# Attention output: weights as the stationary operand, with ones beside the values

## The chip, the cores and the metric

The kernel runs on one core of a Trainium2 chip. The metric is the device time of one execution in microseconds (us). The core has a matrix engine (TensorE; the profile calls its matmuls PE and its loads of stationary operands PEld), a vector engine (DVE), a scalar engine (ACT), GpSimd (POOL) and DMA queues, of which nearly all work here is issued by SP. Each engine executes its own instructions strictly in the order in which the program lists them, and waits on semaphores for what it needs from the others.

## The reference

One layer of a hybrid encoder runs over two requests, a prompt of 256 tokens and a sample of 2048, each with 1024 features. A projection feeds two mixers, a Hyena mixer (two long convolutions by transforms, 512 channels) and a dilated attention (8 heads of 64). Their outputs are normalised, concatenated and projected; then comes a gated feed-forward layer. The change touches the attention, which runs three branches over the same queries, with dilations 1, 4 and 16, and merges them by their softmax denominators:

```
s = jnp.einsum('brnqhe,brnkhe->brnhqk', qb, kb).astype(jnp.float32) * (E ** -0.5)
...
s = jnp.where(valid[None, None, :, None], s + bias[None, None, None], NEG_INF)
m = jnp.max(s, axis=-1, keepdims=True)
p = jnp.exp(s - m)
den = jnp.sum(p, axis=-1)
o = jnp.einsum('brnhqk,brnkhe->brnqhe', p, vb.astype(jnp.float32)) / jnp.swapaxes(den, -1, -2)[..., None]
lse = jnp.swapaxes(m[..., 0] + jnp.log(den), -1, -2)
...
wts = jax.nn.softmax(jnp.stack(lses, axis=0), axis=0)
o = jnp.sum(wts[..., None] * jnp.stack(outs, axis=0), axis=0)
```

So for every query, head and branch three things are needed: the unnormalised sum of weights times values (64 numbers), the extreme score `m`, and the denominator `den`.

## The kernel before

The stages follow each other: input projection and Hyena filters, Hyena with the rest of the projection, attention woven with Hyena, output projection, feed-forward. `mixers` (lines 1052 to 1118) writes attention and Hyena as two generators and `weave` alternates their steps by the rates in line 1050 (`at=440`, `h2=90`). That fixes the order in which the code is emitted. The context is built with `schedule_with_timeline_sim=True` (line 1690): a scheduler then reorders what was emitted, by its own estimate of when each instruction can start, and lists one static order per engine. The order that an engine really executes can therefore move wherever an instruction is added, removed or judged cheaper.

Attention works on pairs of heads (`hp`, four of them), three branches (`b`) and blocks of 128 queries: 54 blocks per pair, 216 in all. One block goes through these steps:

- `scores` (line 874): four matmuls (lines 902, 903; two heads, a high and a low part of the queries) write scores `aS` in PSUM; DVE adds the bias and finds the minimum (line 906; the scores are negated); ACT takes the exponential into `aP` (line 909), and with `accum_out` also the denominator.
- `flip` (line 912): TensorE transposes the weights (line 918, tile `aT`), DVE or ACT copies them to `aPT`.
- `values` (line 928): for each head, the values (`aV`, 64 columns) are the stationary operand and the transposed weights, 128 columns, are moved past them (line 933). The two heads write the lower and upper 64 partitions of `aOp`. A block whose window has two chunks of keys takes four matmuls, one with one chunk two; each fp32 matmul shows as two records in the profile, so 1408 in all.
- After the last block of a group of up to four, ACT copies `aOp` to `aOC` (line 938), `tokens` (line 942) transposes it back to query rows on TensorE (line 946), DVE copies them to `aO` (line 947), and a DMA stores `aO` with minimum and denominator in columns 128 to 131.

Two chunks are of 128 keys each, except at the two ends of a sequence or residue class: there one of the two has 64. There are 88 blocks with two full chunks, 48 with a full and a half one, and 80 with one chunk.

Hyena (line 748) runs its second stage, `hyena_second` (line 696), in 32 steps per convolution of the sample: three fp32 matmuls of 512 columns (lines 721, 725, 739), five DVE operations (lines 723, 729 to 732), a POOL addition (733) and an ACT copy (742). Then 16 steps of the last stage follow (lines 769 to 783): load `hD` from DRAM, two matmuls side by side (line 776, two records each), one DVE multiplication (777), store of the result. All 16 of these steps must be done before the second 256 token rows of the output projection can start, because each step writes rows that are spread over the whole sample. The first 256 rows (the prompt) do not need them.

`merged_rows` (line 1121) later loads the stored rows and merges the branches; `om` (lines 206 to 208 there) is the output projection.

Of the kernel before, what the change touches and what calls it, by code (L numbers as in the profile page):

```python
# [13 lines left out]
F32 = mybir.dt.float32  # L14
F32R = mybir.dt.float32r
AF = mybir.ActivationFunctionType
# [12 lines left out]
REQ = ((0, LP), (LP, LS))  # L29
DILS = (1, 4, 16)  # L30


# [155 lines left out]
class Hybrid:  # L188
# [607 lines left out]
    def attention_groups(self, b, rs):  # L796

        dil = DILS[b]
        out = []
        for r in rs:  # L800
            off, L = REQ[r]
            ls = L // dil
            if ls >= 256:
                nb = ls // P
                out += [(r, "win", [(res, j, nb) for j in range(j0, min(nb, j0 + 4))])
                        for res in range(dil) for j0 in range(0, nb, 4)]
            elif ls == P:
                out += [(r, "res", [(res, 0, 1) for res in range(g, g + 4)]) for g in range(0, dil, 4)]
            else:
                out.append((r, "pack", [(0, j, L // P) for j in range(L // P)]))  # L810
        return out

    def attention_values(self, wp, b, cs):

        nc = self.nc
        dil = DILS[b]
        vt = wp.tile([P, 22, P], F32, tag="aV", name="aV", bufs=2)
        av = self.tok["av"][:, cs]
# [3 lines left out]
        for r in (1, 0):  # L822
# [20 lines left out]
            else:  # L843
                ld(vt[:, n:n + 2], av[off:off + L].rearrange("(p s) k -> p s k", s=2))
                n += 2
        return vt, base

# [22 lines left out]
    def attention(self, wp, psS, psT, psO, first, mq):  # L870
        nc, a = self.nc, self.a
        q1, q2, q3 = [], [], []

        def scores(heads, g, i, blk, ot, bias, b):
# [4 lines left out]
            ps = psS.tile([P, 2, 256], F32, tag="aS", name="aS")  # L879
            sb = wp.tile([P, 2, 256], F32, tag="aP", name="aP", bufs=2)  # L880
            for hh in range(2):
# [22 lines left out]
            for hh in range(2):  # L904
                mn, dn = ot[:, i, 128 + hh:129 + hh], ot[:, i, 130 + hh:131 + hh]
                nc.vector.tensor_tensor_reduce(out=sb[:, hh, :n], in0=ps[:, hh, v0:v0 + n],  # L906
                                               in1=bias[:, hh, b0:b0 + n], scale=1.0, scalar=3e38,
                                               op0=ALU.add, op1=ALU.min, accum_out=mn)
                nc.scalar.activation(sb[:, hh, :n], sb[:, hh, :n], AF.Exp, scale=-1.0, bias=mn, accum_out=dn)  # L909
            return sb, n  # L910
# [16 lines left out]

        def values(x):
            po, vt, i, pe, ch = x["po"], x["vt"], x["i"], x["pe"], x["ch"]
            for c, (c0, cn) in enumerate(ch):  # L930
                for hh in range(2):
                    hs = slice(64 * hh, 64 * hh + 64)
                    nc.tensor.matmul(po[hs, i], vt[:cn, x["v"] + c * x["vs"], hs], pe[:cn, hh, c],
                                     start=(c == 0), stop=(c == len(ch) - 1))
            if x["last"]:
                n = i + 1
                oc = wp.tile([P, 4, P], F32, tag="aOC", name="aOC", bufs=1)
                nc.scalar.copy(oc[:, :n], po[:, :n])
                x["oc"] = oc
                q3.append(x)  # L940

        def tokens(x):
            ot, n = x["ot"], x["i"] + 1
            pt = psT.tile([P, 4, P], F32, tag="aT", name="aOT")
            for i in range(n):
                nc.tensor.transpose(pt[:, i], x["oc"][:, i], self.ident)
            nc.vector.tensor_copy(ot[:, :n, 0:P], pt[:, :n])
            x["store"]()

# [34 lines left out]
        for hp in range(4):  # L984
# [6 lines left out]
            for b in range(3):  # L991
# [6 lines left out]
                for g in self.attention_groups(b, (0, 1) if hp == 3 else (1, 0)):  # L998
                    r, kind, blks = g
                    ot = wp.tile([P, 4, 132], F32, tag="aO", name="aO", bufs=3)  # L1000
                    po = psO.tile([P, 4, P], F32, tag="aOp", name="aOp")
                    for i, blk in enumerate(blks):
# [15 lines left out]
                        if len(q1) > 1:  # L1018
# [3 lines left out]
                            yield  # L1022
                        if q3:
                            tokens(q3.pop(0))
                        if len(q2) > 1:
# [6 lines left out]
        for y in q2:  # L1032
            values(y)
            while q3:
                tokens(q3.pop(0))
        op = self.pool(mq, "o_b", side="left")
# [84 lines left out]
    def merged_rows(self, wp, mg, c0):  # L1121
# [5 lines left out]
        for i in range(2):  # L1127
            rows = slice(c0 + i * P, c0 + (i + 1) * P)
            O = wp.tile([P, 3, 4, 132], F32, tag="oO", name="oO", bufs=2)
            for b in range(3):  # L1130
# [4 lines left out]
            g = wp.tile([P, 4, 2], F32, tag="og", name="og", bufs=2)  # L1135
            mn, dn = O[:, :, :, 128:130], O[:, :, :, 130:132]
            v.tensor_tensor(out=g, in0=mn[:, 0], in1=mn[:, 1], op=ALU.min)
# [10 lines left out]
            for b in range(3):  # L1148
                v.tensor_tensor(out=s[:, b], in0=s[:, b], in1=g, op=ALU.mult)
                ob = O[:, b, :, 0:128].rearrange("p h (k e) -> p h k e", k=2)  # L1150
                wb = s[:, b].unsqueeze(3).broadcast_to([P, 4, 2, 64])
                v.tensor_tensor(out=av if b == 0 else ob, in0=ob, in1=wb, op=ALU.mult)  # L1152
                if b:
                    nc.gpsimd.tensor_tensor(out=av, in0=av, in1=ob, op=ALU.add)
            junk = O[:, 0, :, 0:128]
            nc.scalar.activation(junk, hy.rearrange("p (h e) -> p h e", h=4), AF.Square, accum_out=ss[:, 2 * i:2 * i + 1])
# [538 lines left out]
```

## Time and profile before

| what | value |
| --- | --- |
| median of 3 runs | 3499.14 us (3492.24 to 3500.33) |
| the profiled execution | 3498.32 us, its span 3496.5 us |
| PE busy | 3267.9 us (93%) |
| PEld busy | 2932.6 us (84%) |
| DVE busy | 2492.7 us (71%) |
| ACT busy | 1594.6 us (46%) |
| POOL busy | 1264.4 us (36%) |

The span is the time from the first to the last instruction of the profiled execution. A busy share counts the time in which at least one instruction of the engine was under way, and the ends of matmuls are modelled, so that a full PE may still have small gaps between its matmuls: the distance from one start to the next tells more than the durations, which overlap.

### The profile page before, as it was taken

The page shows a single profiled execution, that of the slowest core. Times are in us where ns is not written, and L with a number is a line of the kernel's source. Part 1 is how long each engine was busy: PE and PEld are TensorE (multiplying, and loading weights), DVE is VectorE, ACT ScalarE, POOL GpSimd, SP SyncE. Part 2 cuts the span into 40 slices and gives each one's busy share as a digit, 9 for nine tenths or more (in the row PEclk, how much of TensorE's full clock was granted, in tenths as well). Part 3 has the DMA queues.
Part 4 walks back from the last instruction along what each step waited for, and adds up shares of the span by engine and source line. Part 5 has one row for each costly group of instructions (what it writes and reads, how often), then busy time and mean ns, then how long its engine had stood idle before and what let it go on. Part 6 is the DMA issues. An engine that isn't in the chain of part 4 may idle for free.

```text
span 3496.5 us, 57581 instructions
## 1 busy us (share of the span) xinstructions
PE 3267.9 (93%) x21142; PEld 2932.6 (84%) x21142; DVE 2492.7 (71%) x4314; ACT 1594.6 (46%) x3322; POOL 1264.4 (36%) x934
## 2 busy tenths in 40 slices
PE   6999899899889899999799899999999999899998
PEld 4987788889756676566789799999999999899998
DVE  7988878665487657685887766767766667467657
ACT  4576753323264655455455433334333334344433
POOL 1487761123231322220454433334533334123222
PEclk9999999999999999999999999999999999999999
DMA  6454457676675766658676623445444224456655
GB/s 243 133 171 130 147 181 235 217 238 200 186 223 174 211 191 197 199 188 249 185 219 182 203 96 129 147 149 198 171 157 143 86 96 148 171 191 226 210 187 176
DMA packets 407825, 628.05 MB, mean 180 GB/s; under 512 B 27919, under 2 KB 230927, under 8 KB 401623
## 3 DMA queue, kind: packets, MB, share of 16 engines
q1 hardware_dynamic: 354384, 593.13, 52.2%
q10 hardware_dynamic: 52072, 28.40, 2.8%
q8 instruction: 167, 2.74, 0.3%
q0 software_dynamic: 1088, 2.85, 0.2%
q14 instruction: 114, 0.93, 0.1%
HBM read 419.03 MB, written 205.25 MB: 179 GB/s over the span
## 4 chain that ended last, share of the span: by engine, by line
PE 40%; DVE 5%; issue 2%; DMA 2%; ACT 1%; POOL 1%; ACTq 0%; SPq 0%; DVEq 0%; POOLq 0%
PE w L208 8%; PE w L207 8%; PE w L206 8%; PE fd L208 4%; PE fd L207 4%; PE fd L206 4%; DVE fT L1260 1%; PE om L208 1%; PE om L207 1%; PE om L206 1%; DVE hl L201 0%; DMA d_x1T<-ox 0%; DMA hl<-d_opT 0%; DMA wraw<-in_w_gate 0%; DVE oO L1152 0%
## 5 line engine op out<-in xcount | busy, mean ns | idle before, releaser
L206 PE MATMUL w<-hh,whi 128*128 128x290 f32 (+1 forms) x2464 | 734.6, 299 | 16.6 <-ACT whi L1354 9.4
L208 PE MATMUL w<-hh,wlo 128*128 128x290 f32 (+1 forms) x2464 | 730.6, 298 | 11.3 <-POOL wlo L201 7.2
L207 PE MATMUL w<-hl,whi 128*128 128x288 f32 (+1 forms) x2464 | 733.8, 298 | 3.9 <-DVE hl L201 3.9
L206 PEld LDWEIGHTS w<-hh,whi 128*128 128x128 f32 x2464 | 469.1, 191 | 19.3 <-ACT whi L1354 11.0
L208 PEld LDWEIGHTS w<-hh,wlo 128*128 128x128 f32 x2464 | 468.0, 190 | 13.5 <-POOL wlo L201 8.1
L207 PEld LDWEIGHTS w<-hl,whi 128*128 128x128 f32 x2464 | 470.8, 191 | 5.5 <-DVE hl L201 5.4
L207 PE MATMUL pj<-hTlo,wihi 128*128 128x386 f32 (+1 forms) x1152 | 401.8, 349 | 7.9 <-DVE hTlo L201 7.9
L206 PE MATMUL pj<-hThi,wihi 128*128 128x386 f32 (+1 forms) x1152 | 403.1, 350 | 5.3 <-ACT u L627 3.2
L208 PE MATMUL pj<-hThi,wilo 128*128 128x386 f32 (+1 forms) x1152 | 398.9, 346 | 0.3 <-DVE wilo L201 0.3
L206 PE MATMUL fd<-hh,dwh 128*128 128x288 f32 x1210 | 360.3, 298 | 12.5 <-ACT dwh L1560 12.5
L208 PE MATMUL fd<-hh,dwl 128*128 128x288 f32 x1210 | 359.1, 297 | 0.0
L207 PE MATMUL fd<-hl,dwh 128*128 128x288 f32 x1210 | 358.0, 296 | 0.0
L733 POOL TENSOR_TENSOR ht<-ht,ht 128x512 f32<-128x512 f32 x72 | 94.6, 1314 | 445.7 <-DVE ht L732 375.8
L206 PEld LDWEIGHTS fd<-hh,dwh 128*128 128x128 f32 x1210 | 230.0, 190 | 13.2 <-ACT dwh L1560 12.7
L207 PEld LDWEIGHTS pj<-hTlo,wihi 128*128 128x128 f32 x1152 | 222.4, 193 | 20.5 <-DVE hTlo L201 9.8
L206 PEld LDWEIGHTS pj<-hThi,wihi 128*128 128x128 f32 x1152 | 221.7, 193 | 16.2 <-issue 4.0
L208 PEld LDWEIGHTS pj<-hThi,wilo 128*128 128x128 f32 x1152 | 221.8, 193 | 13.6 <-issue 8.6
L207 PEld LDWEIGHTS fd<-hl,dwh 128*128 128x128 f32 x1210 | 229.6, 190 | 0.4
L208 PEld LDWEIGHTS fd<-hh,dwl 128*128 128x128 f32 x1210 | 228.1, 189 | 0.1
L909 ACT ACTIVATE aP<-aP,aO 128x256 f32<-128x256 f32 (+2 forms) x432 | 194.1, 451 | 55.4 <-DVE aO L906 46.3
L201 POOL TENSOR_TENSOR wlo<-ws,whi 128x512 fp32r<-128x512 f32 x88 | 133.0, 1511 | 231.1 <-ACT whi L1354 231.1
L1354 ACT CAST whi<-ws 128x512 fp32r<-128x512 f32 x176 | 109.0, 620 | 230.2 <-PE w L207 186.8
(300 smaller groups left out, 7980.6 us busy)
## 6 DMA issues: line engine op xcount, KB each, us to landing
hl<-d_G SPq DMA_DIRECT2D x154, 288.0 KB, 5.2
dwl<-d_S SPq DMA_DIRECT2D x59, 704.0 KB, 4.1
wiraw<-in_w_in SPq DMA_DIRECT2D x72, 512.0 KB, 4.5
d_G<-cv SPq DMA_DIRECT2D x42, 576.0 KB, 2.9
wraw<-in_w_gate SPq DMA_DIRECT2D x22, 1024.0 KB, 4.9
wraw<-in_w_up SPq DMA_DIRECT2D x22, 1024.0 KB, 6.4
adat<-in_ada_t SPq DMA_DIRECT2D x36, 512.0 KB, 4.6
d_fA<-fae SPq DMA_DIRECT2D x72, 256.0 KB, 2.8
```

Of the source, the lines that this page charges most:

```text
L201: eng.tensor_tensor(out=lo, in0=x, in1=hi.bitcast(F32), op=ALU.subtract)
L206: mm(out, wh, xh, start=first, stop=False, skip_group_check=more)
L207: mm(out, wh, xl, start=False, stop=False, skip_group_check=more)
L208: mm(out, wl, xh, start=False, stop=last, skip_group_check=more)
L733: nc.gpsimd.tensor_tensor(out=t1, in0=t1, in1=t2, op=ALU.add)
L909: nc.scalar.activation(sb[:, hh, :n], sb[:, hh, :n], AF.Exp, scale=-1.0, bias=mn, accum_out=dn)
L1260: v.tensor_tensor(out=o, in0=x, in1=y, op=ALU.subtract)
L1354: nc.scalar.copy(hi, x)
```

## The change

The roles of the two operands are exchanged. The transposed weights (up to 128 keys by 128 queries) become the stationary operand, and 65 columns are moved: the 64 values of a head and a column of ones. The result has queries in its partitions, so that the rows need no transpose, and the column of ones gives the denominator, so that the exponential keeps no running sum. The value tile grows to 130 columns, with ones in columns 0 and 129, which POOL writes each time the tile is reused. A group has up to three blocks, since three times 130 numbers fit one PSUM bank; there are 92 groups in place of 60. `aP` gets three buffers for two and `aO` four for three. The stored row keeps 132 numbers in another arrangement.

```diff
+G = 3
+W = 132
...
-        vt = wp.tile([P, 22, P], F32, tag="aV", name="aV", bufs=2)
+        vo = wp.tile([P, 22, 130], F32, tag="aV", name="aV", bufs=2)
+        nc.gpsimd.memset(vo[:, :, 0:130:129], 1.0)
+        vt = vo[:, :, 1:129]
...
-            sb = wp.tile([P, 2, 256], F32, tag="aP", name="aP", bufs=2)
+            sb = wp.tile([P, 2, 256], F32, tag="aP", name="aP", bufs=3)
...
-                nc.scalar.activation(sb[:, hh, :n], sb[:, hh, :n], AF.Exp, scale=-1.0, bias=mn, accum_out=dn)
+                nc.scalar.activation(sb[:, hh, :n], sb[:, hh, :n], AF.Exp, scale=-1.0, bias=mn)
...
-            for c, (c0, cn) in enumerate(ch):
-                for hh in range(2):
-                    hs = slice(64 * hh, 64 * hh + 64)
-                    nc.tensor.matmul(po[hs, i], vt[:cn, x["v"] + c * x["vs"], hs], pe[:cn, hh, c],
+            for hh in range(2):
+                hs = slice(65 * hh, 65 * hh + 65)
+                for c, (c0, cn) in enumerate(ch):
+                    nc.tensor.matmul(po[:, i, hs], pe[:cn, hh, c], vt[:cn, x["v"] + c * x["vs"], hs],
                                      start=(c == 0), stop=(c == len(ch) - 1))
             if x["last"]:
                 n = i + 1
-                oc = wp.tile([P, 4, P], F32, tag="aOC", name="aOC", bufs=1)
-                nc.scalar.copy(oc[:, :n], po[:, :n])
-                x["oc"] = oc
-                q3.append(x)
-
-        def tokens(x):
-            ot, n = x["ot"], x["i"] + 1
-            pt = psT.tile([P, 4, P], F32, tag="aT", name="aOT")
-            for i in range(n):
-                nc.tensor.transpose(pt[:, i], x["oc"][:, i], self.ident)
-            nc.vector.tensor_copy(ot[:, :n, 0:P], pt[:, :n])
-            x["store"]()
+                nc.scalar.copy(x["ot"][:, :n, 0:130], po[:, :n])
+                x["store"]()
...
-                    ot = wp.tile([P, 4, 132], F32, tag="aO", name="aO", bufs=3)
-                    po = psO.tile([P, 4, P], F32, tag="aOp", name="aOp")
+                    ot = wp.tile([P, G, W], F32, tag="aO", name="aO", bufs=4)
+                    po = psO.tile([P, G, 130], F32, tag="aOp", name="aOp")
...
-            mn, dn = O[:, :, :, 128:130], O[:, :, :, 130:132]
+            mn, dn = O[:, :, :, 130:132], O[:, :, :, 0:130:129]
```

The static order of the engines moves with it. On PE, early in the attention of the first pair of heads (`aS` scores, `aT` transposed weights, `aOp` weights times values, `hs` and `hs2` Hyena), the kernel before lists:

```order
L902 MATMUL aS<-Ks,Qh 128x256
L903 MATMUL aS<-Ks,Ql 128x256
L918 MATMUL aT<-ident,aP 128x128 x4
L721 MATMUL hs2k<-hk,htab 128x512
L933 MATMUL aOp<-aPT,aV 64x128 x4
...
L918 MATMUL aT<-ident,aP 128x128 x4
L946 MATMUL aOT<-ident,aOC 128x128 x4
L933 MATMUL aOp<-aPT,aV 64x128 x8
```

And the changed kernel, at the same blocks (its lines are renumbered: 906, 907 scores, 922 transposes, 938 values, 727 and 741 Hyena):

```order
L906 MATMUL aS<-Ks,Qh 128x256
L907 MATMUL aS<-Ks,Ql 128x256
L938 MATMUL aOp<-aV,aPT 128x65 x4
L922 MATMUL aT<-ident,aP 128x128 x4
L727 MATMUL hs2z<-hx,htab 128x512
L741 MATMUL hs_6930<-ht_6841,htab 128x512
L938 MATMUL aOp<-aV,aPT 128x65 x4
```

The transposes back to rows (`aOT`) are gone, and each `aOp` writes 128 partitions and 65 columns where it wrote 64 and 128.

The second place is where attention ends on PE (`ot` and `om` are the output projection, `hs..<-hD` the last Hyena stage, `hs..<-ht` and `hs2` its second stage). Before, from the last scores on:

```order
L903 MATMUL aS<-Ks,Ql 128x256
L918 MATMUL aT<-ident,aP 128x128 x2
L946 MATMUL aOT<-ident,aOC 128x128 x4
L933 MATMUL aOp<-aPT,aV 64x128 x2
L776 MATMUL hs_14458<-hD,hgi_5119 64x512 x2
...
L776 MATMUL hs_14720<-hD,hgi_5119 64x512 x2
L207 MATMUL om<-oml,ow 128x256
```

In the changed kernel from the last scores on, and, after the dots, at the end of Hyena:

```order
L907 MATMUL aS<-Ks,Ql 128x256
L922 MATMUL aT<-ident,aP 128x128 x4
L727 MATMUL hs2z<-hx,htab 128x512
L723 MATMUL hs2k<-hk,htab 128x512
...
L741 MATMUL hs_13550<-ht_13406,htab 128x512
L778 MATMUL hs_13600<-hD,hgi_5119 64x512 x2
...
L778 MATMUL hs_14512<-hD,hgi_5119 64x512 x2
L1174 MATMUL ot<-ident,ohy 128x128 x4
L1174 MATMUL ot<-ident,oat 128x128 x4
```

Behind the last scores the kernel before lists 10 Hyena matmuls, all of the last stage (5 of its 16 steps). The changed kernel lists 68 there: 36 of the second stage (11 `hs2k`, 12 `hs2z`, 13 `hs..<-ht`) and all 32 of the last stage. Between them stands the output projection of the first 256 rows (192 `om`), and nothing else of the output projection.

## Rows read from the trace of the kernel before

**Rows 1.** Busy time by stretch (columns: first line)

```profile
core 0: us, PE busy (x) PEld busy (x) DVE busy (x) ACT busy (x) POOL busy (x), PEclk, DMA share, GB/s
957.00:1300.00 343.00, 322.84 (x1874) 216.55 (x1874) 246.76 (x744) 197.91 (x632) 95.95 (x69) 0.99 0.68 198
1300.00:1640.00 340.00, 323.45 (x1835) 212.54 (x1835) 238.13 (x719) 181.72 (x596) 70.69 (x51) 0.98 0.67 205
1640.00:1660.00 20.00, 11.56 (x47) 6.31 (x46) 13.29 (x20) 9.73 (x18) 8.08 (x5) 0.66 1.04 306
1640.00:1682.00 42.00, 19.12 (x96) 13.30 (x95) 33.70 (x61) 20.81 (x39) 16.34 (x10) 0.67 0.82 235
1585.00:1660.00 75.00, 66.47 (x373) 42.34 (x372) 42.48 (x156) 39.62 (x134) 8.54 (x5) 0.91 0.88 264
```

**Rows 2.** Waits of 957 to 1640 us: total us, times, longest

```profile
DVE aP L906 <- PE aT L918: 64.3, 52, 3.5
...
PEld aOp L933 <- issue: 43.5, 196, 0.8
```

**Rows 3.** Groups by line, 957 to 1640 us: busy us, mean ns, idle

```profile
L933 PE MATMUL aOp<-aPT,aV 128*64 128x128 f32 (+1 forms) x1408 | 136.1, 294 | 3.8 <-ACT aPT L922 3.3
...
L909 ACT ACTIVATION_READ_ACCUMULATOR aP<-aP,aO 128x1 f32 x432 | 81.6, 189 | 0.0
...
L729 DVE TENSOR_TENSOR ht<-hs2z,hK 64x512 f32<-64x512 f32 x58 | 39.5, 680 | 39.6 <-PE hs2z L725 39.2
...
L946 PE MATMUL aOT<-ident,aOC 128*128 128x128 f32 x213 | 34.6, 280 | 2.0 <-ACT aOC L938 1.3 <-ACT aPT L922 0.2 <-DVE aPT L922 0.2
```

**Rows 4.** PE in order of time: start, us, engine, line, what, count

```profile
1200.03 0.81 PE L933 MATMUL aOp<-aPT,aV 128*64 128x128 f32 x8
1200.76 0.61 PE L902 MATMUL aS<-Ks,Qh 128*128 128x256 f32 x1
...
1209.17 0.44 PE L933 MATMUL aOp<-aPT,aV 64*64 64x128 f32 x4
1209.54 0.44 PE L946 MATMUL aOT<-ident,aOC 128*128 128x128 f32 x2
...
1212.69 0.66 PE L933 MATMUL aOp<-aPT,aV 128*64 128x128 f32 x8
1213.28 0.44 PE L918 MATMUL aT<-ident,aP 128*128 128x128 f32 x2
```

**Rows 5.** PE in order of time: scores with 192 moving columns

```profile
1010.34 0.27 PE L902 MATMUL aS<-Ks,Qh 128*128 128x192 f32 x1
1010.45 0.28 PE L903 MATMUL aS<-Ks,Ql 128*128 128x192 f32 x1
```

**Rows 6.** PE in order of time: transposes of 2 columns

```profile
41.46 0.66 PE L285 MATMUL adat<-ident,adar 2*128 2x2 f32 x8
```

**Rows 7.** The same line: ns min/median/max, first and last start

```profile
L285 PE MATMUL adat<-ident,adar x12: 195/196/222, 41.5 to 42.4; 2*128 2x2 f32 x12
```

**Rows 8.** PE in order of time: Hyena matmuls and the output projection

```profile
1064.16 1.02 PE L739 MATMUL hs<-ht,htab 128*128 128x512 f32 x2
1065.02 0.60 PE L918 MATMUL aT<-ident,aP 128*128 128x128 f32 x4
...
1355.52 0.59 PE L721 MATMUL hs2k<-hk,htab 128*128 128x512 f32 x1
...
1562.55 0.59 PE L721 MATMUL hs2k<-hk,htab 128*128 128x512 f32 x1
...
1574.71 0.59 PE L739 MATMUL hs<-ht,htab 128*128 128x512 f32 x1
...
1585.13 0.65 PE L776 MATMUL hs<-hD,hgi 128*64 128x512 f32 x2
...
1657.42 1.25 PE L776 MATMUL hs<-hD,hgi 128*64 128x512 f32 x4
...
1681.52 0.56 PE L206 MATMUL om<-omh,ow 128*128 128x256 f32 x1
```

More of the change, by code (lines that the diff above doesn't have):

```diff
@@ L804, in attention_groups @@
                 nb = ls // P
-                out += [(r, "win", [(res, j, nb) for j in range(j0, min(nb, j0 + 4))])
-                        for res in range(dil) for j0 in range(0, nb, 4)]
+                out += [(r, "win", [(res, j, nb) for j in range(j0, min(nb, j0 + G))])
+                        for res in range(dil) for j0 in range(0, nb, G)]
             elif ls == P:
-                out += [(r, "res", [(res, 0, 1) for res in range(g, g + 4)]) for g in range(0, dil, 4)]
+                out += [(r, "res", [(res, 0, 1) for res in range(g, min(dil, g + G))]) for g in range(0, dil, G)]
             else:
@@ L845, in attention_values @@
                 n += 2
-        return vt, base
+        return vo, base
     def qk_tiles(self, pool, bufs):
@@ L871, in attention @@
         nc, a = self.nc, self.a
-        q1, q2, q3 = [], [], []
+        q1, q2 = [], []
         def scores(heads, g, i, blk, ot, bias, b):
@@ L904, in scores @@
             for hh in range(2):
-                mn, dn = ot[:, i, 128 + hh:129 + hh], ot[:, i, 130 + hh:131 + hh]
+                mn = ot[:, i, 130 + hh:131 + hh]
                 nc.vector.tensor_tensor_reduce(out=sb[:, hh, :n], in0=ps[:, hh, v0:v0 + n],
@@ L1022, in attention @@
                             yield
-                        if q3:
-                            tokens(q3.pop(0))
                         if len(q2) > 1:
@@ L1033, in attention @@
             values(y)
-            while q3:
-                tokens(q3.pop(0))
         op = self.pool(mq, "o_b", side="left")
@@ L1128, in merged_rows @@
             rows = slice(c0 + i * P, c0 + (i + 1) * P)
-            O = wp.tile([P, 3, 4, 132], F32, tag="oO", name="oO", bufs=2)
+            O = wp.tile([P, 3, 4, W], F32, tag="oO", name="oO", bufs=2)
             for b in range(3):
@@ L1149, in merged_rows @@
                 v.tensor_tensor(out=s[:, b], in0=s[:, b], in1=g, op=ALU.mult)
-                ob = O[:, b, :, 0:128].rearrange("p h (k e) -> p h k e", k=2)
+                ob = O[:, b, :, 1:129].rearrange("p h (k e) -> p h k e", k=2)
                 wb = s[:, b].unsqueeze(3).broadcast_to([P, 4, 2, 64])
@@ L1154, in merged_rows @@
                     nc.gpsimd.tensor_tensor(out=av, in0=av, in1=ob, op=ALU.add)
-            junk = O[:, 0, :, 0:128]
+            junk = O[:, 0, :, 1:129]
             nc.scalar.activation(junk, hy.rearrange("p (h e) -> p h e", h=4), AF.Square, accum_out=ss[:, 2 * i:2 * i + 1])
```

## The prediction

> **What bounds the kernel now.** I first read busy time by stretch. Attention runs from 957 to 1640 us of the span, and PE is busy for 322.84 of 343 and 323.45 of 340 us of it, at a granted clock of 0.99 and 0.98 of 2.4 GHz; DVE has 485 of the 683 us, ACT 380, POOL 167 [rows 1]. So PE is the engine that sets this stage, with 37 us of idle time that can be seen. The table also shows what comes behind it: from 1640 to 1682 us PE works 19.12 of 42 us, at a clock of 0.67 (between the two levels, so part of the time at 1.2 GHz). That is a passage between two stages, in which a chain sets the end, not an engine. Then the waits inside the stage: the longest that the change touches is DVE waiting 64.3 us for a transpose, because the scores' buffer `aP` is not free; and the load of the values waits 43.5 us in 196 pieces for nothing that the profile names [rows 2]. Then the groups by line, for counts, and last PE in order of time, where the distance between starts gives the price of an instruction.
>
> **Weights times values on PE.** A group of 8 records (two heads, two chunks, two records each) starts at 1212.69 and the next operation at 1213.28: 0.59 us. With one chunk it is 4 records in 0.37 us; with a full and a half chunk, 8 records in 0.73 us [rows 4]. If r is the time of a record and g what is lost at the end of a group, 8r + g = 0.59 and 4r + g = 0.37 give r = 0.055 and g = 0.15. The 128 moving columns of the two heads run side by side, which makes r so small. With 88, 48 and 80 blocks of the three kinds the groups cost 51.9 + 35.0 + 29.6 = 116.5 us (the groups by line have 136.1 us, in which the ends of matmuls are modelled [rows 3]).
>
> After the change there are again 1408 records, as before [rows 3]. Each moves 65 columns past a stationary operand 128 columns wide, and no longer has a neighbour beside it. The trace has no such fp32 record. The nearest row is the scores' matmul with 192 moving columns: 0.11 us from start to start [rows 5]. I read this as the time of loading 128 stationary columns, behind which a shorter stream hides. From below there are transposes of two columns with 128 stationary ones, 8 in 0.66 us of which the last takes 0.196: 0.066 each [rows 6, 7]. From above, load and stream in a row: 0.11 for the load and 0.055 for the 65 columns (before, 128 columns of a single head take twice 0.055, and 65 are half), so 0.165. I take 0.111, the row that has a full array and no transposes, so 1408 x 0.111 = 156 us. The 48 blocks with a half chunk now change between 64 and 128 rows four times, where I charge 0.1 us each (under g, which also holds an exposed load): 19 us. Sum 175, that is 58 us more.
>
> The Trainium skill, "TensorE: Matmul & The Clock Gate", Part 3, "What overlaps and what doesn't", says that a load of stationary columns overlaps matmuls under way only where the row group differs. Here all 128 rows are the same group, so by that rule load and stream would add. This trace speaks against it without settling it: 192 columns and a full load together in 0.11 us leave little room for a sum. The rule is carried below as a rival, and its price is that of the upper bound.
>
> What goes from PE: 216 transposes back to rows (213 of them recorded [rows 3]), at 0.11 us a piece: four of the other transposes span 0.60 us [rows 8], of which the last takes 0.28 as the mean of line 946 does, and (0.60 - 0.28) / 3 is 0.107. That is 24 us. The change of the array's shape into and out of a group, outside the 48 mixed ones: going out is in the 0.59 and 0.37 above; going in is the wait of 43.5 us in 196 pieces, 0.22 each [rows 2], of which the stream before it covers about half, so 168 x 0.1 = 17 us. The operation behind such a group loads late: a first scores' matmul lasts 0.61 us there [rows 4], one in a stream 0.28 [rows 5]; part of this is its longer and strided operand, so I count 0.15 for half of the groups, 90 cases, 13 us (an estimate). Together 54 us less. So PE's own bill stays as it was: +58 - 54 = +4 us.
>
> **Beside the path.** ACT loses 432 reads of an accumulator, 81.6 us [rows 3], and DVE 60 copies; both engines have room in this stage, so alone they give nothing. ACT's copies out of `aOp` become 92 smaller ones. POOL gets 12 fills of ones, in front of the loads of `aV`: it has 516 us of room in the stage, but a fill queues behind Hyena's additions, and the value loads of a branch queue behind the fill; I price this between 0 and 12 x 2 us and take nothing, since the fill stands a branch ahead. The third `aP` buffer takes away much of the 64.3 us wait of DVE. What of that reaches PE is at most the 37 us of visible idle time; I take 10.
>
> **What the new order does.** This is where I see the cost. The order shows that Hyena falls back against attention: 68 of its matmuls stand behind the last scores, where it was 10. 36 of these are of the second stage, two records of 0.43 us each ((1065.02 - 1064.16) / 2 [rows 8]): 31 us. The other 22 are 11 more steps of the last stage; the four records of a step run in pairs side by side, so they cost like two of the second stage, 0.9 with the change of shape, and the four at 1657.42 span 1.25 at a lower clock [rows 8]; I count 1.0 each, 11 us. So attention is relieved of 42 us and ends at 1640 + 4 - 42 - 10 = 1592 us.
>
> But then Hyena must be finished, alone. The second stage has 12 of 32 steps left. In the kernel before 31 steps take from 1355.52 to 1562.55, 6.7 us each, with attention beside them [rows 8]; the floor is five DVE operations of 0.68 [rows 3], 3.4 us. Free of attention I take 4.2: 50 us (41 to 80). The 192 matmuls of the first 256 output rows, the only other work there, take 23 us of PE and fit in. From the last second stage matmul to the first of the last stage, through DRAM: 1585.13 - 1574.71 = 10 us [rows 8]. Then 16 steps, each with 512 KB loaded, 256 KB of gate loaded and 256 KB stored, 16.8 MB in all. Before, these steps run from 1585 to 1660 us with the DMA engines at 0.88 and 264 GB/s; the best 20 us have 306 GB/s [rows 1]. That gives 55 to 64 us, and before they took 73; I take 60. From the last of these matmuls to the second 256 output rows: 1681.52 - 1657.42 = 24 us [rows 8]. Sum 144 us, so the output projection goes on at 1592 + 144 = 1736 us where it was 1681.5. What follows is the same code and the same bill. 54.5 us later, from the profiled execution's 3498.3 (span 3496.5, and 1.8 around it; the median of the runs, 3499.1, is 0.8 above): **3553 us**.
>
> **Rivals.** (1) Short loads. If a record takes 0.066, as the transposes of two columns do, attention ends 1408 x 0.045 = 63 us earlier and the time is 3490; the change is then not slower. It decides from 0.072 a record (54.5 / 1408 = 0.039 below 0.111). For it: the only row with so few moving columns. Against it: those are transposes of two partitions, and 0.11 stands in rows with a full array. (2) Load and stream add, 0.165 a record: 1408 x 0.054 = 76 us more, 3629. For it the skill's rule, against it the 0.11 of 192 columns. (3) The forecast's mechanism, but a cheap tail: PE loses all its 37 us of idle time, and the tail runs at its floor, 41 + 10 + 55 + 24 = 130: 3553 - 27 - 14 = 3512. The dear end of the same: no idle time won and 80 + 10 + 73 + 24 = 187: 3553 + 10 + 43 = 3606. (4) The change does not do what it says: the order shows the transposes gone, so only a tail that hides behind other work would leave 3499; nothing but 23 us of it is listed there.
>
> **How the numbers follow.** The forecast with its two ends has 0.70, its own range 3512 to 3606. Short loads have 0.14, added load and stream 0.12, a hidden tail 0.04. The range reaches from 3490, the short loads, to 3612, the dear end and a little for DMA. A measurement of this kernel can tell 0.3% (10.5 us) from no change. Faster by more than that needs loads as short as 0.066 and some idle time won: 0.10. The same: the rest of the short loads and the hidden tail, 0.08. Slower: 0.82.
>
> **What would show it.** In the profile after: (a) line 938, 4 or 8 records with 0.11 us from start to start, and no wait of 0.17 before each group; 0.066 or 0.165 would show a rival. (b) No `aOT`, no read of an accumulator on ACT. (c) Attention's last matmul near 1592 us, and PE fuller than 95% until then. (d) Behind it some 140 us in which Hyena works on, PE is idle for more than half of the time and the granted clock falls, DMA is near full in the last 60, and the second block of `om` starts near 1736. (e) From there to the end the same time as before, 1815 us. If `om` goes on before 1700 us, the forecast is wrong, and I would look at the pace of Hyena's steps first.

## The result and the profile after

The changed kernel takes 3559.10 us, the median of 4 runs (3556.18 to 3565.03); the kernel before took 3499.73 us beside it (4 runs, 3492.24 to 3505.98). The ratio is 1.0173 (95% interval 1.0149 to 1.0197), some 60 us more. The forecast was 3553. The profiled execution took 3565.03 us, its span is 3562.9.

By stretch, as in [rows 1] (columns: stretch, length, busy time and count of each engine, granted clock, DMA share, GB/s):

```profile
957.00:1300.00 343.00, 328.02 (x1777) 262.24 (x1776) 229.78 (x705) 183.01 (x434) 88.51 (x67) 0.95 0.65 187
1300.00:1592.00 292.00, 284.21 (x1593) 231.52 (x1592) 190.81 (x630) 157.17 (x388) 72.37 (x55) 0.98 0.59 178
1592.00:1673.00 81.00, 61.58 (x279) 38.86 (x278) 61.21 (x101) 19.21 (x33) 26.75 (x23) 0.89 0.65 201
1673.00:1738.00 65.00, 32.12 (x65) 4.76 (x64) 10.38 (x15) 0.58 (x1) 0.00 (x0) 0.50 0.76 242
1738.00:1755.00 17.00, 4.58 (x21) 3.80 (x20) 5.85 (x8) 6.00 (x14) 1.75 (x1) 0.50 0.60 188
```

Attention ends 48 us earlier, at 1592. But behind it stand 162 us in which Hyena finishes, the last 82 of them at half clock. The output projection goes on at 1754 instead of 1682, 73 us later. Multiplying PE's busy time by the granted clock tells what these 73 us are. From 957 on, the kernel before has 665 us busy, 649 of full-clock work, in 725 us; the changed one 711 busy, 663 of work, in 798. So 28 us are more idle time, 31 are lower clock and 14 are more work. Summed piece by piece over the trace, with the clock unrounded, it is the same 28, 31 and 14. The 14 us are no dearer attention: the stretch now holds 142 more matmuls of the output projection (17 us at 0.12), as the rows further down show. Like for like PE's work is 3 us less.

The values product in the timeline of PE (start, duration, engine, line, operation, shapes, count), three groups with the operation behind each, as in [rows 4]:

```profile
958.96 1.53 PE L938 MATMUL aOp<-aV,aPT 64*128 64x65 f32 x8
960.32 0.61 PE L922 MATMUL aT<-ident,aP 128*128 128x128 f32 x4
...
1589.84 1.00 PE L938 MATMUL aOp<-aV,aPT 128*128 128x65 f32 x8
1590.67 0.28 PE L922 MATMUL aT<-ident,aP 128*128 128x128 f32 x1
...
1592.25 0.56 PE L938 MATMUL aOp<-aV,aPT 128*128 128x65 f32 x4
1592.64 1.12 PE L741 MATMUL hs<-ht,htab 128*128 128x512 f32 x2
```

Eight full records (128 rows) take 0.83 us, four 0.39: 0.11 a record, with nothing lost at the group's end. A block with a half chunk takes 1.36. By these prices the 216 blocks cost 170 us, where I had 175. The waits of the same stretch (engine, line, whom it waited for: us in total, times, longest), against [rows 2]:

```profile
DVE aP L910 <- PE aS L907: 43.4, 41, 3.1
PEld aOp L938 <- issue: 20.1, 73, 0.8
```

DVE no longer waits 64 us for a transpose to free `aP`, but for scores; the load of the stationary operand has lost half of its unexplained wait. The end of Hyena, in PE's timeline:

```profile
1671.60 2.07 PE L741 MATMUL hs<-ht,htab 128*128 128x512 f32 x2 [5.94 <-POOL ht L735]
1681.38 1.98 PE L778 MATMUL hs<-hD,hgi 128*64 128x512 f32 x4 [7.70 <-DMA hD<-d_hB]
...
1736.18 1.98 PE L778 MATMUL hs<-hD,hgi 128*64 128x512 f32 x4 [1.09 <-DVE hg L779]
1749.60 1.12 PE L1174 MATMUL ot<-ident,ohy 128*128 128x128 f32 x4 [11.45 <-DVE ohy L1159]
...
1754.34 1.01 PE L208 MATMUL om<-omh,ow 128*128 128x256 f32 x3
```

The same place of the kernel before corrects a reading of mine. The prediction took the `om` at 1681.52 in [rows 8] for the start of the second 256 rows:

```profile
1664.09 0.28 PE L208 MATMUL om<-omh,ow 128*128 128x256 f32 x1
1676.76 1.09 PE L1183 MATMUL ot<-ident,ohy 128*128 128x128 f32 x4 [12.39 <-DVE ohy L1168]
...
1690.93 0.28 PE L206 MATMUL om<-omh,owh 128*128 128x256 f32 x1
```

What waits for Hyena is the transposes `ot` of the second block; about 50 of the first block's 192 `om` matmuls stand before them in PE's order and 142 behind. At 1681.52 the first block went on (`owh`, the later weights, come at 1690.93). In the changed kernel the first block is done within Hyena's tail, by 1658, and 1754.34 is the second block. So the rest after this point could have become shorter by 17 us; it did by 6 (1815 to 1808.6). Measured to the same place, the second block's first `om` (1701.3 before, 1754.3 now), PE is 53 us late: 28 of idle time, 30 of lower clock, and 4 us less work. Behind it another 13 us are lost: 6 of idle time, 10 of clock, 2 less of work.

### The profile page after: what moved, and what is told of

Read it like the earlier page. It is cut to its first block, busy times and chain, and to the rows that moved or that the text cites. A ratio compares the mean times of both kernels' runs of the same rounds, so it can differ in the third digit from the quotient of the medians.

```text
span 3562.9 us, 56859 instructions
## 1 busy us (share of the span) xinstructions
PE 3303.1 (93%) x20926; PEld 3020.3 (85%) x20926; DVE 2465.5 (69%) x4254; ACT 1561.9 (44%) x2926; POOL 1255.2 (35%) x946
## 4 chain that ended last, share of the span: by engine, by line
PE 58%; DVE 7%; DMA 7%; issue 2%; ACT 2%; SPq 1%; POOL 1%; ACTq 0%; DVEq 0%; POOLq 0%
PE w L210 8%; PE w L208 8%; PE w L209 8%; PE fd L210 4%; PE fd L209 4%; PE fd L208 4%; PE aOp L938 4%; PE aS L906 2%; PE aS L907 2%; PE aT L922 2%; PE hs2k L723 1%; PE hs2z L727 1%; PE hs L741 1%; PE pj L209 1%; PE pj L208 1%
## 5 line engine op out<-in xcount | busy, mean ns | idle before, releaser
L208 PE MATMUL w<-hh,whi 128*128 128x288 f32 (+1 forms) x2464 | 735.4, 299 | 16.3 <-ACT whi L1345 9.9
L938 PEld LDWEIGHTS aOp<-aV,aPT 128*128 128x128 f32 (+1 forms) x1408 | 193.9, 196 | 52.5 <-issue 20.3
L210 PEld LDWEIGHTS pj<-hThi,wilo 128*128 128x128 f32 x1152 | 220.9, 192 | 12.2 <-issue 8.0
L910 DVE CUSTOM_DVE_ANT_0 aP<-aS,aB 128x256 f32<-128x256 f32 (+2 forms) x432 | 136.2, 355 | 115.6 <-PE aS L907 43.4
```

The costliest lines, as they stand in the source:

```text
L208: mm(out, wh, xh, start=first, stop=False, skip_group_check=more)
L210: mm(out, wl, xh, start=False, stop=last, skip_group_check=more)
L938: nc.tensor.matmul(po[:, i, hs], pe[:cn, hh, c], vt[:cn, x["v"] + c * x["vs"], hs], start=(c == 0), stop=(c == len(ch) - 1))
```

## The experiments

Theory A is that of the prediction: the operand swap costs PE nothing on balance, and the loss is that Hyena falls back and must finish alone. Theory B: the values product itself (or the buffers that came with it) is the loss. Ratios are against runs of the kernel before on the same chip.

**e1_out2**, the changed kernel with two output buffers:

```
-                    ot = wp.tile([P, G, W], F32, tag="aO", name="aO", bufs=4)
+                    ot = wp.tile([P, G, W], F32, tag="aO", name="aO", bufs=2)
```

> The changed kernel with two output buffers aO instead of four. In its PE order no Hyena matmul stands behind the last scores, where the changed kernel has 68. Theory A (the loss is the Hyena tail, PE's own bill for attention is nearly unchanged): Hyena's 42 us go back among attention, which then ends near 1634 us instead of 1592, and the second block of om starts at most 42 us later as in the kernel before, near 1658 to 1676 instead of 1754. Time 3462 to 3500, if two buffers make PE wait by up to 18 us. Theory B (the loss is the dearer values product on PE, the tail is only where it shows): the time stays at 3545 to 3565.

Measured: 3577.62 us, ratio 1.0217 (1.0202 to 1.0233). Neither number came. The tail is gone, but attention now lasts until 1731. Its stretches, and its new wait:

```profile
957.00:1300.00 343.00, 307.37 (x1589) 230.14 (x1587) 220.37 (x620) 159.36 (x371) 93.46 (x73) 0.95 0.65 189
1300.00:1597.00 297.00, 271.47 (x1324) 200.54 (x1324) 195.53 (x558) 133.79 (x317) 72.25 (x55) 0.91 0.63 186
1597.00:1666.00 69.00, 63.44 (x300) 41.38 (x300) 24.43 (x92) 21.71 (x55) 0.16 (x1) 0.81 0.84 257
1666.00:1731.00 65.00, 53.98 (x295) 49.09 (x294) 26.09 (x135) 33.91 (x93) 6.41 (x5) 0.84 0.21 60
```

```profile
DVE aP L910 <- DMA d_O<-aO: 67.2, 33, 8.1
```

Busy times clock, it is 636 us of full-clock work, and the kernel before has 637 up to the end of its attention at 1640. So PE has no more work (against B), and the 91 us by which attention ends later are 41 of idle time and 51 of lower clock: DVE waits for the stores of `aO`, PE for DVE. The order was repaired at the price of a stall; I had allowed 18 us for it.

**e2_weights2**, `aP` with `bufs=2` instead of 3.

> The changed kernel with two weight buffers aP, as the kernel before has, instead of three. 34 Hyena matmuls stand behind the last scores: two of the second stage and all 32 of the last stage. Theory A: the 34 others (29 us of PE) go before the end of attention, which moves from 1592 to some 1621 us, later by up to 10 if DVE waits for aP again; behind it stand 9 us of turn, 56 us of last stage and 17 us of restart as in the changed kernel, so om goes on at 1703 to 1713 instead of 1754, time 3508 to 3518. Theory B: 3545 to 3565.

Measured: 3551.44 us, ratio 1.0134 (1.0115 to 1.0153): between the two. Attention ends at 1650, where I expected 1621 to 1631: against the changed kernel's 1592 that is 36 us more work (29 of them Hyena's that came back), 16 of idle time and 7 of clock. The last stage then takes 79 us, since the first `om` block falls beside it, with DMA at 0.90. It does not tell A from B.

**e3_before_late**, the kernel before with Hyena woven in later:

```
-    RATES = dict(p1=42, f=90, ad=36, h1=135, p2=39, h2=90, at=440)
+    RATES = dict(p1=42, f=90, ad=36, h1=60, p2=39, h2=90, at=440)
```

> The kernel before, with its values product, its transposes of the output rows and its buffers, but with Hyena woven into the projection at less than half the rate (60 instead of 135), so that it falls back: 39 of its matmuls stand behind the last scores, all 32 of the last stage among them, where it was 10. Theory A: attention ends about 17 us earlier, near 1623, and then stand 10 us of second stage, 9 of turn, 56 of last stage and 17 of restart: om goes on at 1710 to 1728 instead of 1681.5, time 3527 to 3546 without any change of the operands. Theory B (the tail costs little by itself, the loss is the values product): 3495 to 3510.

Measured: 3554.16 us, ratio 1.0154 (1.0135 to 1.0174): +54 us without any change of operands, a little over A's range and far from B. PE's timeline shows the same passage as the changed kernel's:

```profile
1633.94 0.44 PE L933 MATMUL aOp<-aPT,aV 128*64 128x128 f32 x4
...
1638.31 1.13 PE L739 MATMUL hs<-ht,htab 128*128 128x512 f32 x2
...
1654.04 1.97 PE L776 MATMUL hs<-hD,hgi 128*64 128x512 f32 x4 [6.94 <-DMA hD<-d_hB]
```

Its last stage ends at 1727 and the second block of `om` starts at 1742.9, 109 us behind attention's end (162 in the changed kernel, 62 in the kernel before); attention ends only 5 us earlier than there, not 17 as expected. So a late Hyena costs this much without the change.

**e4_wide**, twice the moving columns in the values product:

```
-                    nc.tensor.matmul(po[:, i, hs], pe[:cn, hh, c], vt[:cn, x["v"] + c * x["vs"], hs],
+                    nc.tensor.matmul(po[:, i], pe[:cn, hh, c], vt[:cn, x["v"] + c * x["vs"]],
...
```

> The changed kernel, but each matmul of the values product moves 130 columns (both heads' values and both columns of ones) instead of 65; the second head's product overwrites that of the first, so half of the result is left out. Twice the stream, the same stationary operand, the same count of records. 60 Hyena matmuls behind the last scores. Theory L (a record's 0.111 us is the time to load its 128 stationary columns, the stream hides behind it): 0.111 us a record again, time 3545 to 3565. Theory S (load and stream stand in a row, each about half of 0.111): 0.165 a record, 1408 x 0.054 = 76 us more of PE, time 3610 to 3640.

Measured: 3561.09 us, ratio 1.0171 (1.0156 to 1.0186), theory L. In the trace of this kernel:

```profile
960.58 1.74 PE L937 MATMUL aOp<-aV,aPT 64*128 64x130 f32 x8
962.16 0.60 PE L922 MATMUL aT<-ident,aP 128*128 128x128 f32 x4
...
967.08 1.06 PE L937 MATMUL aOp<-aV,aPT 128*128 128x130 f32 x8
967.98 0.60 PE L922 MATMUL aT<-ident,aP 128*128 128x128 f32 x4
```

In a run of full records one starts 0.112 us behind the other, with 130 columns as with 65: the longer stream hides behind the rest of the record, which I read as its load (no run varied the stationary columns). Only one longer stream in each run does not hide: eight records take 0.90 in place of 0.83. A block with a half chunk grew from 1.36 to 1.58, and there load and stream do add. Record by record, two with the same rows start 0.161 us apart with 65 columns and 0.215 with 130, which is the time of 65 more columns; this holds for the two full records of such a block as for the two with 64 rows. Each change between 64 and 128 rows takes 0.20 in both kernels.

That the whole time equals that of 65 columns is partly luck. By these prices the 130 columns cost PE some 19 us more (48 x 0.22 and some 160 x 0.054), and the clock gave as much back: from 957 to 1592 the lower clock takes 25 us of PE's busy time in the changed kernel and 6.5 in this one. Theory S's 76 us are out all the same. The same 60 us, first of the changed kernel, then of this one:

```profile
1197.00:1257.00 60.00, 60.00 (x326) 51.52 (x325) 24.40 (x105) 27.45 (x72) 11.13 (x10) 0.91 0.45 133
```

```profile
1197.00:1257.00 60.00, 60.00 (x338) 49.48 (x338) 25.27 (x106) 27.81 (x72) 11.20 (x10) 1.00 0.45 133
```

PE is busy all the time in both, yet the granted clock is 0.91 with 65 columns and 1.00 with 130.

**e5_pace**, the test of A without touching a buffer. `STEPS` holds how many Hyena matmuls the kernel before issues between the blocks of attention:

```
+    def keep_pace(self, mm):
+        n = sum(int(c, 36) for c in self.STEPS[:len(self.blocks)]) + 125
+        self.blocks.append(mm)
+        if n <= len(self.hpe):
+            self.tc.add_manual_dep(mm.ins, self.hpe[n - 1].ins.name, mybir.DependencyInfo(
+                mybir.DependencyClass.NoSync, mybir.DependencyReason.DATA), reason="pace")
...
```

The rate `h2` of the weave is raised as well, from 90 to 145, here and in e6, e8, e9, e11 and e12; what that does alone was not run.

> The changed kernel with edges of order on PE (no waits): the first scores' matmul of each block stands behind as many Hyena matmuls as in the kernel before, so that 10 of them are left behind the last scores instead of 68. Buffers and operands are those of the change. Theory A (the loss is that Hyena fell back and its end stands alone): attention ends at 1640 to 1655 us, om goes on at 1682 to 1700, time 3495 to 3517. Theory B (the values product or the buffers cost the time on PE): 3540 to 3565. Theory C (beside A, the granted clock is lower among the records of 65 columns: 0.94, 0.96 and 0.98 in the three stretches from 957 to 1592 us, where the kernel before has 0.98, 0.98 and 0.99; some 15 us): 3510 to 3530.

Measured: 3513.86 us (6 runs, 3506.89 to 3526.56), ratio 1.0038 (1.0024 to 1.0052). Order, with the same operands and buffers, gives back 47 of the 60 us: A, and against B. In the profiled execution, the slowest of the six, attention ends at 1675 and `om` goes on at 1717, later than A's 1640 to 1655 and 1682 to 1700. That points to C:

```profile
957.00:1300.00 343.00, 318.08 (x1672) 248.98 (x1671) 223.41 (x672) 171.43 (x402) 90.17 (x71) 0.93 0.65 192
1300.00:1640.00 340.00, 322.98 (x1657) 245.35 (x1656) 218.66 (x646) 159.66 (x382) 77.47 (x60) 0.94 0.62 189
```

Idle time is 42 us, as before (37), but the clock is 0.93 and 0.94 where it was 0.99 and 0.98. Over the six runs the time follows the mean granted clock of the whole run: 3526.6 at 0.964, 3522.1 at 0.967, 3514.4 at 0.969, 3513.3 at 0.970, 3506.9 at 0.972, 3509.1 at 0.973.

**e6_pace_wide**, e5 with the 65 columns moved twice:

```
+                    va = vt[:cn, x["v"] + c * x["vs"], hs].unsqueeze(1).broadcast_to([cn, 2, 65])
+                    nc.tensor.matmul(po[:, 130 * i + 65 * hh:130 * i + 65 * hh + 130], pe[:cn, hh, c], va,
...
```

> The kernel of e5_pace, but each matmul of the values product moves its 65 columns twice (130 columns by a broadcast; the second copy lands on columns that the next product overwrites), so that the result is the same and the records still take 0.11 us. Theory C: the granted clock in attention goes back to 0.98 or more, as in e4_wide, and the time is 8 to 20 us below e5_pace. Against it: the clock is set by the gaps between PE's instructions alone, and the 64-row records grow from 0.16 to 0.215 us (192 x 0.054 = 10 us): 0 to 12 us above e5_pace.

Measured: 3518.77 us (5 runs, 3508.75 to 3519.44), ratio 1.0046 (1.0034 to 1.0058). The clock does come back (the profiled execution is the fastest of the five):

```profile
957.00:1300.00 343.00, 322.55 (x1706) 249.42 (x1706) 227.33 (x681) 172.04 (x409) 93.88 (x72) 0.98 0.65 190
1300.00:1640.00 340.00, 322.42 (x1698) 243.53 (x1697) 223.45 (x677) 161.14 (x394) 76.08 (x58) 0.99 0.66 203
```

The time does not fall: as in e4, the 130 columns cost PE about what the clock gives. The account behind e11 has the numbers.

**e7_before_buffers**, the kernel before with `aP` of three buffers and groups of three blocks.

> The kernel before with the change's groups of three blocks and its three weight buffers aP, and nothing else of the change (operands, transposes of the rows and the sums of the weights on ACT stay). In its order no Hyena matmul stands behind the last scores (10 in the kernel before). Theory A: what DVE waits for aP (64 us) goes, PE gets at most the 37 us of its idle time, and the tail is no longer than before: 3480 to 3505. Rival (more buffers let attention run ahead and Hyena falls back on the chip, whatever the order says): 3520 to 3560.

Measured: 3519.48 us, ratio 1.0053 (1.0041 to 1.0065): neither theory, though the time just misses the rival's range. Hyena did not fall back; attention was the one left behind, and PE waited more for DVE (first scores' matmul 19.8 us, 5.9 in the kernel before). So groups of three and the third buffer together cost some 19 us there, by another mechanism than the changed kernel's.

**e8_pace_lead**, `n` plus one for every twentieth block.

> The kernel of e5_pace with a growing lead for Hyena: one matmul more before every twentieth block, so that all of Hyena stands before the last scores. Theory A: the 24 us from the last Hyena matmul to the second block of om pass beside attention's end, om goes on up to 20 us earlier than in e5_pace, and the time is 5 to 20 us below it. Rival (Hyena's chain can't go faster beside attention; PE then stands before a Hyena matmul whose operand isn't there): 0 to 30 us above e5_pace.

Measured: 3538.51 us, ratio 1.0111 (1.0098 to 1.0124): the rival. PE stands before Hyena matmuls whose operands are not loaded (L683 is the helper that issues them):

```profile
PE hs2k L683 <- DMA hk<-d_fA: 15.7, 10, 4.6
PE hs L683 <- DMA hD<-d_hB: 11.5, 5, 9.1
PE hs2z L683 <- DMA hx<-d_hA: 8.4, 6, 3.8
```

**e9_tail_alone**: is the second stage slow because of what runs beside it?

```
+        with self.tc.issue_after(self.hdve.ins):
+            self.first_rows = self.merged_rows(op, mg, 0)
...
+            with self.tc.issue_after(self.hpe.ins):
+                nxt = self.merged(wp, psp, self.first_rows)
```

> The changed kernel, in which the first block of rows for the output projection (its sums on DVE, its transposes and om on PE) must stand behind the last second-stage step of Hyena, by edges of order. So Hyena's second stage runs out alone behind attention: 14 steps by the order, 12 in the changed kernel. There the tail took 80 us, 6.6 a step, where I had predicted 50 (4.2 a step). Theory D (om's loads and DVE work beside it stretch the steps: DMA had a share near 0.9 there): 3.6 to 4.6 us a step, the 14 steps within 50 to 65 us of attention's end. Rival (the step's own chain of loads, DVE, POOL and PE takes 6 to 7 us whatever runs beside it): 85 to 98 us. The whole time tells little, since om's first block is only moved behind (3545 to 3575).

Measured: 3578.50 us, ratio 1.0203 (1.0180 to 1.0226). The 14 steps take 84 us, 6.0 each: near the rival, far from D. Each pair of steps starts with an `hs2z`; the SP line is the last load that is not Hyena's own:

```profile
1597.48 2.05 PE L727 MATMUL hs2z<-hx,htab 128*128 128x512 f32 x2 [2.08 <-DMA hx<-d_hA]
...
1612.83 2.04 PE L727 MATMUL hs2z<-hx,htab 128*128 128x512 f32 x2 [0.58 <-DMA hx<-d_hA]
...
1620.23 0.55 SPq L1209 DMA_DIRECT2D ox<-in_xD  x1
...
1628.87 1.10 PE L727 MATMUL hs2z<-hx,htab 128*128 128x512 f32 x2 [1.47 <-DMA hx<-d_hA]
...
1639.51 1.02 PE L727 MATMUL hs2z<-hx,htab 128*128 128x512 f32 x2
...
1647.24 2.05 PE L723 MATMUL hs2k<-hk,htab 128*128 128x512 f32 x2 [2.11 <-issue]
...
1652.65 1.02 PE L727 MATMUL hs2z<-hx,htab 128*128 128x512 f32 x2
...
1663.93 1.28 PE L727 MATMUL hs2z<-hx,htab 128*128 128x512 f32 x2
```

So Hyena is alone only from about 1629 on. There a pair takes 10.6, 13.1 and 11.3 us, 5.3 to 6.6 a step, with a DMA share of 0.45 to 0.51. The two pairs before take 15.4 and 16.0 us, 7.7 to 8.0 a step: beside them run the loads of the output weights and of `ox` (DMA share 0.78 and 0.94) and five DVE operations on those weights. The chain by itself is thus well above the 4.2 us that I had predicted, and D holds for a part of the tail; which of the loads and the DVE operations stretches the steps was not separated.

**e12_tail_hk2**, e9 with `hk` of two buffers (and one less of `ht1` and of `aPT`):

> The kernel of e9_tail_alone with two buffers hk for the filter rows of Hyena's second stage instead of one (room for it from one buffer less of ht1 and of aPT). In e9 the second stage, alone, went on at 13.1 us for each pair of steps: hk is loaded 1 us after the pair's last matmul that reads it, lands 5.5 us later, and only then the next pair begins. Theory K (the single buffer makes load and steps stand in a row): the load hides, a pair takes 13.1 - 5.5 = 7.6 us, bounded by DVE's ten operations of 0.69 us, so 3.5 to 4.5 a step. Rival (the chain through hx, POOL and PE of a slower clock holds it): 5.5 to 6.6 a step. The order has some 10 steps behind attention where e9 has 14. Whole time: with K 3535 to 3560, else 3560 to 3580.

Measured: 3547.92 us, ratio 1.0145 (1.0119 to 1.0171). The whole time lies in K's range, but fewer steps stand behind the last scores than in e9 (11 against 14), so it says little. Pairs start at 1608.88, 1623.28, 1635.46 and 1646.69. The first two, of 14.4 and 12.2 us, again run beside the loads of the output weights and of `ox`; the third takes 11.2, 5.6 a step. That is the rival's: K's 7.6 us a pair did not come, and against e9's 10.6 to 13.1 the second buffer shows no gain (a cost of the `ht1` buffer that went is not separated). What holds the pair is the chain itself:

```profile
1635.46 1.10 PE L727 MATMUL hs2z<-hx,htab 128*128 128x512 f32 x2 [0.78 <-DMA hx<-d_hA]
...
1639.54 1.90 PE L727 MATMUL hs2z<-hx,htab 128*128 128x512 f32 x2 [2.12 <-DVE ht L734]
1641.23 1.92 PE L723 MATMUL hs2k<-hk,htab 128*128 128x512 f32 x2
...
1645.73 1.12 PE L741 MATMUL hs<-ht,htab 128*128 128x512 f32 x2 [1.69 <-POOL ht L735]
1646.69 1.02 PE L727 MATMUL hs2z<-hx,htab 128*128 128x512 f32 x2
```

The first step of the pair takes 4.1 us, as I had priced all of them. The second takes 7.2: in PE's order the next pair's `hs2z` stands behind this pair's last `hs`, which waits for four DVE operations and POOL's addition.

**e10_before_om**, an attempt at a faster kernel before: the second block's `ot` behind more of the first block's `om`.

```
+                    if not c0 and m == 4:
+                        with self.tc.issue_after(self.mlast.ins):
+                            nxt = self.merged(wp, psp, rows)
```

> The kernel before with one edge of order in the output projection: the transposes of the second block of rows, which wait for Hyena's last rows (PE idle for 12.4 us there), stand behind the fifth of the eight output tiles of the first block instead of behind the second. Some 70 om matmuls (8.4 us at 0.12) can fill the wait. If PE's order is what costs there: 5 to 9 us less than the kernel before, 3490 to 3495. Rival (the sums and loads of the second block set the pace behind it anyway): 3497 to 3502.

Measured: 3506.18 us, ratio 1.0011 (1.0002 to 1.0019): no gain, 4 us more if anything. The wait only moved to the `om` matmuls, whose output tile DVE had not emptied:

```profile
1678.84 0.58 PE L206 MATMUL om<-omh,ow 128*128 128x256 f32 x1 [16.67 <-DVE ox L1228]
```

**e11_pace_wide_om**, e6 with 65 columns in all records of the blocks that have a half chunk, the full ones among them, and with this edge.

> The kernel of e6_pace_wide, with 130 moving columns only where all 128 rows are used (the 64-row records keep 65 columns, 0.16 instead of 0.215 us, 192 x 0.054 = 10 us less), and with the edge of e10_before_om. Theory C (order, clock and the 64-row records are all that the change loses): 3519 - 10 - 7 = 3502, 3496 to 3508. Rival (the clock falls with the 65-column records that are left, or e6 won nothing by its clock): 3510 to 3520.

Measured: 3523.80 us, ratio 1.0062 (1.0049 to 1.0074). A miss: even without the 4 us of the edge it is no faster than e6. No version here beats the kernel before.

**An account over the runs.** From 957 us to the first `om` of the second block every kernel does the same part of the program. In that stretch of each profiled execution, work is PE's busy time multiplied piece by piece by the granted clock, the clock's column is what the busy time exceeds it by, and the rest is idle. Kernels with the same work come out between 655 and 671 us over all runs here, so that a difference in work of less than 10 us tells little by itself.

| run | profiled us | stretch | work | idle | clock |
| --- | --- | --- | --- | --- | --- |
| before | 3498.3 | 744.3 | 665.3 | 59.8 | 19.2 |
| changed | 3565.0 | 797.3 | 661.2 | 87.5 | 48.7 |
| e3_before_late | 3550.4 | 785.9 | 668.5 | 90.7 | 26.8 |
| e4_wide | 3561.0 | 797.0 | 680.0 | 86.0 | 31.0 |
| e7_before_buffers | 3519.5 | 769.2 | 658.7 | 80.9 | 29.5 |
| e5_pace | 3526.6 | 774.4 | 662.8 | 63.5 | 48.2 |
| e6_pace_wide | 3508.8 | 757.7 | 682.3 | 62.3 | 13.2 |
| e11_pace_wide_om | 3523.8 | 765.4 | 672.0 | 70.0 | 23.3 |

The order of before takes the idle time back (e5), and nearly all that e5 still loses in its profile, 29 of 30 us, is clock. The six runs agree: their median of the mean granted clock is 0.9695, against 0.974 for the kernel before beside them, and 0.0045 of 3500 us is some 16 us (an estimate), where the times differ by 15. The groups and buffers of e7, the other candidate, cost mostly idle time there, which e5 does not have. The 130 columns get the clock back (e4 against the changed kernel, e6 against e5), but cost 19 us of work, and 9 in e11, where only the blocks without a half chunk have them; the prices of single records under e4 give the same. So e6 and e11 were no test of whether the clock costs the last 13 us: they paid for it with about as much work as they won. Where these 13 us go is thus read from the traces; why the clock is lower among the records of 65 columns stays open.

## Why the prediction was right, and where it was off

- **Values record.** Forecast 0.111 us, measured 0.11; the half-chunk block 1.29 and 1.36. The row it came from, the scores' matmul, is of another kind (one record for a matmul, not two), so that the two agree was not a given. Rival 1 (0.066) and rival 2 (0.165) are out by the timeline, and e4 shows that in a run of full records a stream of up to 130 columns hides behind the rest of the record. The rule of the Trainium skill that rival 2 drew on ("TensorE: Matmul & The Clock Gate", Part 3, "What overlaps and what doesn't": overlap only where the row group differs) would forbid this for records that use all rows; the trace has 0.11 for 65 as for 130 columns. In blocks that change between 64 and 128 rows load and stream did add, 0.161 and 0.215 us apart, for full records too.
- **PE's bill.** Forecast +4 us, measured 3 to 4 less, with some 8 open by the account above. Right within that.
- **Attention's end.** Forecast 1592, measured 1592.5, partly by luck: PE has 47 us less work up to there (I took 38), the idle time fell by 14 us (37 to 23; I took 10), and 13 us that I had not foreseen went to the clock (25 us lost against 12).
- **The tail.** Second stage 50 us forecast, 80 measured: the mis-sized term, though the bounds of 41 to 80 held it. I divided by DVE's work and took the cover of attention for the brake; e9 and e12 show a chain of 5.3 to 6.6 us a step with nothing beside it, and 6.1 to 8.0 beside the loads of the output weights and of `ox`, which I had left out. The turn took 9 us (10), the last stage 56 (60), the restart 17 (24). The sum is 162, not 144.
- **What follows.** Forecast unchanged, measured 6 us shorter; the row at 1681.52 was misread, as shown above, so that the 24 us of restart and the start of the rest were not what I took them for. So 3553 + 18 - 6 gives the profiled 3565.
- **The mechanism** is shown from both sides: the order of before in the changed kernel gives 47 us back (e5), and a late Hyena costs the kernel before 54 (e3). Rival 4 is out. The lower clock in attention was in no term of the sum; by the account above it holds what e5 still loses.

## What to carry to other kernels

Where two streams share one engine and a scheduler lists the order by its own estimate, relieving one stream moves the other back; count what stands behind the last instruction of the relieved one, and price it as a chain, link by link and with the loads of the next stage beside it, not by its busiest engine. Test such a cause with edges of order, not with fewer buffers: those repaired the order as well, but brought stalls of their own (e1 ended above the changed kernel, e2 only some 10 us below it). And where two kernels take the same time, compare the price of single records before calling their work equal: in e4 a dearer product and a better clock cancelled out.

## What was not expected of the hardware

The granted clock fell to 0.91 from 1197 to 1257 us with PE busy in all 60 us, among records that move 65 columns in 0.11 us; with 130 columns in the same records it stayed at 1.00 there. And whether load and stream of a record overlap depends on the records around it: in a run of full records they start 0.112 us apart with 65 columns as with 130, but in a block that changes between 64 and 128 rows two records of the same rows start 0.161 and 0.215 us apart, full ones as well, and each change takes 0.20.
